# A decoder layer in fp32 on one core: the slices of the conditioning matrix get buffers and a queue of their own

## The chip, the cores and the metric

The kernel runs on one NeuronCore of a Trainium2 chip. The metric is the device time of one execution in microseconds (us); lower is better. The engines are TensorE (PE, with its weight loads PEld), VectorE (DVE), ScalarE (ACT), GpSimd (POOL) and SyncE (SP). Each runs its own list of instructions strictly in order, and they wait for one another through semaphores. Transfers between HBM and SBUF run on 16 DMA engines; they are put on a queue by the engine that issues them, here nearly always SP.

## The reference

One decoder layer on 256 tokens of width 2048, all in float32, with a conditioning vector c. What matters here:

```python
mod = silu(c) @ w_ada + b_ada              # 2048 x 12288: shift1, scale1, gate1, shift2, scale2, gate2
h   = RMSNorm(x) * (1 + scale1) + shift1
p   = h @ w_in                             # retention q,k,v,g | HGRN2 q,f,i,g | branch gates A, B
yA  = (LN_head(Retention(rope(q), rope(k), v)) * silu(g)) @ w_ret_o
yB  = (RMS_head(HGRN2(silu(q), f, i)) * silu(g)) @ w_hg_o
x   = x + gate1 * ((sigmoid(gA) * yA + sigmoid(gB) * yB) @ w_out)
h2  = RMSNorm(x) * (1 + scale2) + shift2
u   = causal_depthwise_conv3(h2 @ w_up);  a, b = split(u)
x   = x + gate2 * ((silu(a) * b) @ w_down)
out = RMSNorm_final(x)
```

## The kernel before

**Weights.** Every weight matrix is read once, in pieces of two k-tiles by 512 columns: 128 partitions by 1024 floats, 512 KB. A piece goes through one chain, which is called a weight step below. SP loads it into a buffer `raw` (`load`, L160). ACT rounds it to the format float32r, `wh` (L169). DVE subtracts, `wl = raw - wh` (L174), which ends the use of `raw`. TensorE multiplies with `wh` and `wl` (L191 to L193, L204 to L206, L848 and L849). `wh` and `wl` have four buffers each. The first eight steps, and a few more, have one k-tile (256 KB). There are 536 weight steps, and their order on DVE, ACT, SP and PE is fixed by the program.

**Conditioning.** `w_ada` stands transposed in memory with the bias appended, so that 128 outputs of `mod` are a 128 x 2049 slice, and TensorE has no part in it: DVE multiplies the slice with silu(c), which is kept on all partitions (`sc`), and sums along the row in the same instruction (L380). Each slice is loaded in two halves, of 1024 and of 1025 columns. One half, its load and its multiplication are called a dot here; there are 192 of them, with 100 MB in all: 64 for scale1 and shift1 (`ada1`), 32 for gate1, 64 for scale2 and shift2 (`ada2`), 32 for gate2. Small ACT instructions (L389 to L392, L400) put the two sums together. The halves of a dot use the same buffers `raw` as the weights, eight in all, and the same queue of SP:

```python
raw = self.wp.tile([P, m, w], F32, name=f"raw_{self.n}", tag="raw", bufs=8)   # load, L159
self.pin(self.nc.sync.dma_start(out=raw, in_=src))
```

**Order of the work.** The main program walks through the matrix products: twelve groups of columns of `w_in` for the attention branches (with the dots of `ada1` between them, since h needs them tile by tile), then `wb`, `wab`, `whg`, `wret`, `wout`, then 22 groups of `wup`, then `wdown`. Beside it run generators as background work: the recurrences (`hgrn`, `retention`), `gate_cols` and `ada2`. After each weight step `pump` lets them go on by a share of time that `pace` sets. So in program order gate1 and `ada2` are spread over the stages from `wb` to `wout`, and gate2 over `wup`.

The instructions are not issued in program order, though. While the program is built, a scheduler goes through it and writes the list of each engine: an instruction that has its inputs and a free buffer may be put ahead of others that are waiting, and earlier code has precedence. Only instructions that went through `pin` in the parts marked `ordered` (the start, and the passage from `wout` to the first group of `wup`) keep their program order. Loads on one queue stand in the order in which buffers come free for them.

**POOL** does next to nothing: it clears two tiles of each HGRN2 half, `at` (L486) and `kt` (L510), and issues two loads of `decay` (L593).

Of the kernel before, what the change touches and what calls it, by code (L numbers as in the profile page):

```python
# [12 lines left out]
F32 = mybir.dt.float32  # L13
# [3 lines left out]
ALU = mybir.AluOpType  # L17

P = 128
D = 2048  # L20
T = 256
NT = T // P
KT = D // P
# [9 lines left out]
RESIDENT = 2  # L33
ADA_EVERY = 11
LAG = 1
NOSYNC = mybir.DependencyInfo(mybir.DependencyClass.NoSync, mybir.DependencyReason.DATA)
SMALL = 70

# [4 lines left out]
GW = 2 * G  # L43
# [11 lines left out]
class Kernel:  # L55
    def __init__(self, ctx, tc, a):
        self.tc, self.nc, self.a = tc, tc.nc, a
        self.consts = ctx.enter_context(tc.tile_pool(name="consts", bufs=1))
        self.wp = ctx.enter_context(tc.tile_pool(name="wp", bufs=1))
        self.sb = ctx.enter_context(tc.tile_pool(name="sb", bufs=1))  # L60
        self.ps = ctx.enter_context(tc.tile_pool(name="ps", bufs=1, space=bass.MemoryType.PSUM))

        self.back = [deque(), deque()]
        self.rate = [0.0, 0.0]
        self.credit = [0.0, 0.0]
        self.n = 0

        self.ordered = True
# [87 lines left out]

    def load(self, src, m, w):
        self.n += 1
        raw = self.wp.tile([P, m, w], F32, name=f"raw_{self.n}", tag="raw", bufs=8)  # L159
        self.pin(self.nc.sync.dma_start(out=raw, in_=src))  # L160
        return raw

    def upper(self, src, m, w):
# [207 lines left out]
        self.pin(ins)  # L371
        return ins

    def ada_dot(self, src):

        nc = self.nc
        part = self.small([P, 2], name="dot", bufs=6)
        for u, w in enumerate((GW, D + 1 - GW)):
            raw = self.load(src[:, u * GW : u * GW + w], 1, w)
            self.pin(nc.vector.scalar_tensor_tensor(raw[:, 0, :], raw[:, 0, :], 1.0, self.sc[:, u * GW : u * GW + w], ALU.mult, ALU.mult, accum_out=part[:, u : u + 1]))  # L380
            yield 1.15
        return part

    def scale_shift(self, name, k, sc, sh, gn):

        act = self.nc.scalar.activation
        kk = slice(k, k + 1)
        part = yield from self.ada_dot(self.a[name][k, 0])
        self.pin(act(sc[:, kk], part[:, 0:1], AF.Identity, bias=part[:, 1:2]))  # L389
        self.pin(act(sc[:, kk], gn[:, kk], AF.Identity, bias=gn[:, kk], scale=sc[:, kk]))  # L390
        part = yield from self.ada_dot(self.a[name][k, 1])
        self.pin(act(sh[:, kk], part[:, 0:1], AF.Identity, bias=part[:, 1:2]))  # L392

    def gate_cols(self, name):
        gate = self.consts.tile([P, KT], F32, name=name)
        self.gate[name] = gate
        for k in range(KT):
            kk = slice(k, k + 1)
            part = yield from self.ada_dot(self.a[name][k])
            self.nc.scalar.activation(gate[:, kk], part[:, 0:1], AF.Identity, bias=part[:, 1:2])  # L400

    def ada2(self):
# [236 lines left out]
    def run(self):  # L639
# [12 lines left out]
        def act(k):  # L652
            return hT[k // 2][:, k % 2, :]

        def ada1(k):
            yield from self.scale_shift("ada1", k, s1, t1, self.gn1)
            if k % 2 == 0:
                hT[k // 2] = self.blk([P, 2, 2 * T], F32R, name="hT")
                if k:
                    ins = self.times(k, 2, rx_sb)  # L660
                    self.tc.add_manual_dep(ins.ins, start.ins.name, NOSYNC, reason="after the start")
            self.modulated(act(k), self.xT[k // 4][:, k % 4, :], k, s1, t1)
# [50 lines left out]
        while min(done) < KT:  # L713
            if work > SMALL and not small:
# [3 lines left out]
                self.start(self.lower_bound())  # L718
            have = min(KT, 2 + int((work - LAG) / ADA_EVERY))
            m = have - done[g]  # L720
# [267 lines left out]
```

## Time and profile before

| | before |
|---|---|
| median of 3 runs | 1580.73 us (1579.52 to 1589.53) |
| profiled execution, own time | 1580.22 us |
| its span, first to last instruction | 1578.4 us |
| PE busy | 1545.5 us (98%) |
| DVE busy | 1174.7 us (74%) |
| ACT busy | 839.8 us (53%) |
| POOL busy | 5.2 us |
| moved by DMA | 382.91 MB, 243 GB/s over the span |
| granted TensorE clock | 0.995 |

Busy time is the union of an engine's instructions. An engine that waits shows in the tables as idle time before an instruction, with the engine or transfer that ended the wait. L numbers are lines of the kernel before.

### The profile page before, as it was taken

What the parts mean: (1) busy time and instruction counts of PE and PEld (TensorE: products, weight loads), DVE (VectorE), ACT (ScalarE), POOL (GpSimd) and SP (SyncE); (2) the same over time, 40 slices, a digit from 0 to 9 for tenths busy, and PEclk for the clock granted to TensorE, in tenths of its full rate; (3) what the DMA queues carried; (4) which work ended last, traced back from release to release, by engine and by line L of the source; (5) the groups of instructions that cost most, each with busy time, mean ns of one, the idle gap of its engine ahead of it and who ended that gap; (6) DMA issues with size and microseconds to landing.
All of it is one profiled execution on the core that took longest, in us unless ns stands there. A gap on an engine that the chain in (4) does not pass through costs nothing.

```text
span 1578.4 us, 27236 instructions
## 1 busy us (share of the span) xinstructions
PE 1545.5 (98%) x10804; PEld 1439.9 (91%) x10804; DVE 1174.7 (74%) x1615; ACT 839.8 (53%) x1203; POOL 5.2 (0%) x10
## 2 busy tenths in 40 slices
PE   7999999999999999989999999999999999999997
PEld 6999999888999999989988888888888889999997
DVE  6899986997988866678758777777677768445444
ACT  5655455667755543344446555555555557434342
POOL 0000000000000000000000000000000000000000
PEclk9999999999999999999999999999999999999999
DMA  9999996887876778889847777777676666666661
GB/s 317 338 326 340 323 323 210 273 282 234 274 244 223 258 260 291 270 261 325 324 139 238 234 240 232 228 228 226 222 243 211 225 191 187 176 188 185 183 179 54
DMA packets 110019, 382.91 MB, mean 243 GB/s; under 512 B 12866, under 2 KB 13506, under 8 KB 109892
## 3 DMA queue, kind: packets, MB, share of 16 engines
q1 hardware_dynamic: 109440, 380.31, 74.1%
q8 instruction: 84, 1.38, 0.4%
q0 software_dynamic: 160, 0.79, 0.2%
q14 instruction: 43, 0.35, 0.1%
q10 hardware_dynamic: 292, 0.08, 0.0%
HBM read 379.04 MB, written 2.10 MB: 241 GB/s over the span
## 4 chain that ended last, share of the span: by engine, by line
PE 84%; DMA 7%; DVE 6%; issue 2%; ACT 1%; DVEq 0%; ACTq 0%; SPq 0%
PE pg L848 10%; PE po L848 10%; PE pg L206 9%; PE pg L204 9%; PE pg L205 9%; PE pg L849 5%; PE po L849 5%; DMA raw<-in_ada 5%; PE po L206 4%; PE po L204 4%; PE po L205 4%; PE pg L191 3%; PE pg L192 3%; PE pg L193 3%; DVE wl L174 3%
## 5 line engine op out<-in xcount | busy, mean ns | idle before, releaser
L174 DVE TENSOR_TENSOR wl<-raw,wh 128x1024 fp32r<-128x1024 f32 (+1 forms) x536 | 632.1, 1190 | 217.1 <-ACT wh L169 216.3
L169 ACT ACTIVATE wh<-raw 128x1024 fp32r<-128x1024 f32 (+1 forms) x536 | 544.9, 1029 | 416.6 <-PE pg L205 157.3
L380 DVE SCALAR_TENSOR_TENSOR raw<-raw,sc 128x1024 f32<-128x1024 f32 x192 | 234.2, 1224 | 131.5 <-DMA raw<-in_gate 66.9
L206 PE MATMUL pg<-hT,wl 128*128 128x256 f32 x896 | 254.1, 284 | 2.7 <-DVE wl L174 2.7
L204 PE MATMUL pg<-hT,wh 128*128 128x256 f32 x896 | 256.1, 286 | 0.1
L205 PE MATMUL pg<-hT,wh 128*128 128x256 f32 x896 | 253.5, 283 | 0.0
L848 PE MATMUL pg<-h2T,wh 128*128 128x512 f32 x704 | 247.1, 396 | 1.8 <-DVE h2T L365 1.8
L848 PE MATMUL po<-h2T,wh 128*128 128x512 f32 x704 | 244.6, 394 | 0.0
L849 PE MATMUL pg<-h2T,wl 128*128 128x256 f32 x704 | 196.2, 279 | 0.0
L849 PE MATMUL po<-h2T,wl 128*128 128x256 f32 x704 | 195.0, 277 | 0.0
L206 PEld LDWEIGHTS pg<-hT,wl 128*128 128x128 f32 x896 | 171.7, 192 | 3.7 <-DVE wl L174 3.7
L204 PEld LDWEIGHTS pg<-hT,wh 128*128 128x128 f32 x896 | 172.0, 192 | 1.2 <-ACT wh L169 0.6
L205 PEld LDWEIGHTS pg<-hT,wh 128*128 128x128 f32 x896 | 171.9, 192 | 0.3
L848 PEld LDWEIGHTS pg<-h2T,wh 128*128 128x128 f32 x704 | 133.1, 189 | 33.0 <-DVE h2T L365 2.0
L848 PEld LDWEIGHTS po<-h2T,wh 128*128 128x128 f32 x704 | 132.0, 188 | 30.6
L849 PEld LDWEIGHTS pg<-h2T,wl 128*128 128x128 f32 x704 | 133.3, 189 | 0.1
L849 PEld LDWEIGHTS po<-h2T,wl 128*128 128x128 f32 x704 | 132.2, 188 | 0.0
L191 PE MATMUL pg<-wh,hT 128*128 128x512 f32 x256 | 100.7, 393 | 0.0
L192 PE MATMUL pg<-wl,hT 128*128 128x512 f32 x256 | 100.0, 390 | 0.7 <-DVE wl L174 0.7
L193 PE MATMUL pg<-wh,hT 128*128 128x512 f32 x256 | 99.7, 390 | 0.0
L204 PE MATMUL po<-gs,wh 128*128 128x256 f32 x352 | 99.6, 283 | 0.0
L205 PE MATMUL po<-gs,wh 128*128 128x256 f32 x352 | 99.6, 283 | 0.0
(207 smaller groups left out, 2739.4 us busy)
## 6 DMA issues: line engine op xcount, KB each, us to landing
raw<-in_wup SPq DMA_DIRECT2D x176, 512.0 KB, 4.5
raw<-in_wdown SPq DMA_DIRECT2D x88, 512.0 KB, 3.9
raw<-in_wa SPq DMA_DIRECT2D x80, 512.0 KB, 5.6
raw<-in_ada SPq DMA_DIRECT2D x64, 512.5 KB, 5.4
raw<-in_ada SPq DMA_DIRECT2D x64, 512.0 KB, 5.3
raw<-in_wab SPq DMA_DIRECT2D x64, 512.0 KB, 4.8
raw<-in_gate SPq DMA_DIRECT2D x32, 512.5 KB, 4.3
raw<-in_wb SPq DMA_DIRECT2D x32, 512.0 KB, 5.4
```

Of the source, the lines that this page charges most:

```text
L169: self.pin(self.nc.scalar.activation(wh, raw, AF.Copy))
L174: self.last = self.nc.vector.tensor_tensor(wl, raw, wh.bitcast(F32), ALU.subtract)
L191: nc.tensor.matmul(ps[t], lhsT=hi, rhs=wh, start=first, stop=False)
L192: nc.tensor.matmul(ps[t], lhsT=hi, rhs=wl, start=False, stop=False)
L193: nc.tensor.matmul(ps[t], lhsT=lo, rhs=wh, start=False, stop=last)
L204: nc.tensor.matmul(out, lhsT=wh[:, cs], rhs=hi, start=opens, stop=False, skip_group_check=True)
L205: nc.tensor.matmul(out, lhsT=wh[:, cs], rhs=lo, start=False, stop=False, skip_group_check=True)
L206: nc.tensor.matmul(out, lhsT=wl[:, cs], rhs=hi, start=False, stop=last, skip_group_check=True)
L380: self.pin(nc.vector.scalar_tensor_tensor(raw[:, 0, :], raw[:, 0, :], 1.0, self.sc[:, u * GW : u * GW + w], ALU.mult, ALU.mult, accum_out= ...
L848: nc.tensor.matmul(ps[j], lhsT=wh[:, cs], rhs=act, start=kt == 0, stop=False)
L849: nc.tensor.matmul(ps[j][:, :T], lhsT=wl[:, cs], rhs=act[:, :T], start=False, stop=kt == KT - 1)
```

## The change

The halves of the dots get a pool of their own, `ada`, with three buffers. The pool `raw` has five buffers left, for the weights. The halves are listed ahead by `dot_plan`; when a dot is about to be multiplied, `dot_rows` first issues the loads of the next two, on the queue of GpSimd. In the part marked `ordered` at the start the first eight dots are still loaded by SP, the first half of each slice into a buffer of `raw`, the second into one of `ada`. The multiplication is the same; the lines of the changed kernel are 34 higher in this part (L414 for L380, L208 for L174, L163 and L169 for the loads).

```diff
--- before.py
+++ after.py
@@ -33,6 +33,7 @@
 RESIDENT = 2
 ADA_EVERY = 11
 LAG = 1
+AHEAD = 2
 NOSYNC = mybir.DependencyInfo(mybir.DependencyClass.NoSync, mybir.DependencyReason.DATA)
 SMALL = 70
 
@@ -59,6 +60,8 @@
         self.wp = ctx.enter_context(tc.tile_pool(name="wp", bufs=1))
         self.sb = ctx.enter_context(tc.tile_pool(name="sb", bufs=1))
         self.ps = ctx.enter_context(tc.tile_pool(name="ps", bufs=1, space=bass.MemoryType.PSUM))
+        self.plan = self.dot_plan()
+        self.fetched = deque()
 
         self.back = [deque(), deque()]
         self.rate = [0.0, 0.0]
@@ -156,8 +159,39 @@
 
     def load(self, src, m, w):
         self.n += 1
-        raw = self.wp.tile([P, m, w], F32, name=f"raw_{self.n}", tag="raw", bufs=8)
+        raw = self.wp.tile([P, m, w], F32, name=f"raw_{self.n}", tag="raw", bufs=5)
         self.pin(self.nc.sync.dma_start(out=raw, in_=src))
+        return raw
+
+    def load_dot(self, src, w, engine):
+        self.n += 1
+        raw = self.wp.tile([P, D + 1 - GW], F32, name=f"ada_{self.n}", tag="ada", bufs=AHEAD + 1)[:, :w]
+        self.pin(engine.dma_start(out=raw, in_=src))
+        return raw
+
+    def dot_plan(self):
+
+        for name, n in (("ada1", 2), ("gate1", 0), ("ada2", 2), ("gate2", 0)):
+            for k in range(KT):
+                for i in range(max(n, 1)):
+                    src = self.a[name][k, i] if n else self.a[name][k]
+                    for u, w in enumerate((GW, D + 1 - GW)):
+                        yield (name, k, i, u), src[:, u * GW : u * GW + w], w
+
+    def dot_rows(self, key):
+
+        if self.ordered and not self.fetched:
+            got, src, w = next(self.plan)
+
+            raw = self.load_dot(src, w, self.nc.sync) if got[3] else self.load(src, 1, w)[:, 0, :]
+        else:
+            while len(self.fetched) <= AHEAD:
+                got = next(self.plan, None)
+                if got is None:
+                    break
+                self.fetched.append((got[0], self.load_dot(got[1], got[2], self.nc.gpsimd)))
+            got, raw = self.fetched.popleft()
+        assert got == key, (got, key)
         return raw
 
     def upper(self, src, m, w):
@@ -371,13 +405,13 @@
         self.pin(ins)
         return ins
 
-    def ada_dot(self, src):
+    def ada_dot(self, name, k, i=0):
 
         nc = self.nc
         part = self.small([P, 2], name="dot", bufs=6)
         for u, w in enumerate((GW, D + 1 - GW)):
-            raw = self.load(src[:, u * GW : u * GW + w], 1, w)
-            self.pin(nc.vector.scalar_tensor_tensor(raw[:, 0, :], raw[:, 0, :], 1.0, self.sc[:, u * GW : u * GW + w], ALU.mult, ALU.mult, accum_out=part[:, u : u + 1]))
+            raw = self.dot_rows((name, k, i, u))
+            self.pin(nc.vector.scalar_tensor_tensor(raw, raw, 1.0, self.sc[:, u * GW : u * GW + w], ALU.mult, ALU.mult, accum_out=part[:, u : u + 1]))
             yield 1.15
         return part
 
@@ -385,10 +419,10 @@
 
         act = self.nc.scalar.activation
         kk = slice(k, k + 1)
-        part = yield from self.ada_dot(self.a[name][k, 0])
+        part = yield from self.ada_dot(name, k)
         self.pin(act(sc[:, kk], part[:, 0:1], AF.Identity, bias=part[:, 1:2]))
         self.pin(act(sc[:, kk], gn[:, kk], AF.Identity, bias=gn[:, kk], scale=sc[:, kk]))
-        part = yield from self.ada_dot(self.a[name][k, 1])
+        part = yield from self.ada_dot(name, k, 1)
         self.pin(act(sh[:, kk], part[:, 0:1], AF.Identity, bias=part[:, 1:2]))
 
     def gate_cols(self, name):
@@ -396,7 +430,7 @@
         self.gate[name] = gate
         for k in range(KT):
             kk = slice(k, k + 1)
-            part = yield from self.ada_dot(self.a[name][k])
+            part = yield from self.ada_dot(name, k)
             self.nc.scalar.activation(gate[:, kk], part[:, 0:1], AF.Identity, bias=part[:, 1:2])
 
     def ada2(self):
```

The scheduler makes a new list from this for each engine. The list of PE is the same but for 14 matmuls that stand a few places off. DVE, ACT and POOL have other lists.

On DVE, at the start of the program, the multiplications of the second k-tile of h stood like this before (`wl_291` is the first weight step of that tile, `hT_198` the tile, `raw_285` the last half of a slice that it needs):

```order
L380 SCALAR_TENSOR_TENSOR raw_285,dot_281<-raw_285,sc 128x1025
L370 TENSOR_TENSOR xT_94<-xT_94,rx_sb 128x512 x2
L370 TENSOR_TENSOR xT_95<-xT_95,rx_sb 128x512
L353 TENSOR_TENSOR hT_198<-h_294,hT_198 128x256
L174 TENSOR_TENSOR wl_291<-raw_288,wh_290 128x512
```

In the changed kernel the same place of DVE's list reads:

```order
L414 SCALAR_TENSOR_TENSOR ada_285,dot_281<-ada_285,sc 128x1025
L414 SCALAR_TENSOR_TENSOR ada_387,dot_386<-ada_387,sc 128x1024
L414 SCALAR_TENSOR_TENSOR ada_389,dot_386<-ada_389,sc 128x1025
L387 TENSOR_TENSOR hT_198<-h_294,hT_198 128x256
L208 TENSOR_TENSOR wl_291<-raw_288,wh_290 128x512
```

Two dots of the third k-tile, `ada_387` and `ada_389`, the first that POOL loads, now stand ahead of the weight step `wl_291`.

Further on, on DVE, ahead of the last weight steps of the branch gates (`wl_6533` before is the same step as `wl_6537` in the change, the 205th), the list had dots of `ada2` between the weight steps:

```order
L174 TENSOR_TENSOR wl_6468<-raw_6465,wh_6467 128x1024
L380 SCALAR_TENSOR_TENSOR raw_6659,dot_6625<-raw_6659,sc 128x1025
L174 TENSOR_TENSOR wl_6503<-raw_6500,wh_6502 128x1024
L380 SCALAR_TENSOR_TENSOR raw_6696,dot_6695<-raw_6696,sc 128x1024
L174 TENSOR_TENSOR wl_6533<-raw_6530,wh_6532 128x1024
L380 SCALAR_TENSOR_TENSOR raw_6729,dot_6695<-raw_6729,sc 128x1025
```

In the change the dots at this place are the last of gate2 (`ada_12409` to `ada_12799`), and weight steps alone follow:

```order
L414 SCALAR_TENSOR_TENSOR ada_12409,dot_12685<-ada_12409,sc 128x1024
L208 TENSOR_TENSOR wl_6472<-raw_6469,wh_6471 128x1024
L414 SCALAR_TENSOR_TENSOR ada_12557,dot_12685<-ada_12557,sc 128x1025
L208 TENSOR_TENSOR wl_6507<-raw_6504,wh_6506 128x1024
L414 SCALAR_TENSOR_TENSOR ada_12686,dot_12926<-ada_12686,sc 128x1024
L414 SCALAR_TENSOR_TENSOR ada_12799,dot_12926<-ada_12799,sc 128x1025
L208 TENSOR_TENSOR wl_6537<-raw_6534,wh_6536 128x1024
L208 TENSOR_TENSOR wl_6570<-raw_6567,wh_6569 128x1024
```

So all 192 dots stand ahead of the 205th weight step now; before, 125 of them did, and the last stood between two steps of `wup`. Counted in the two lists, the dots ahead of the 107th weight step are 64 before and 95 in the change; ahead of the 210th they are 128 and 192.

POOL's list, which had only the clearing of `at` and `kt` and the loads of `decay`, has 184 loads of dots now. Where the first HGRN2 half is cleared (`at_3393`, `kt_3480`; dots of `ada2` around them) it reads:

```order
L169 DMA ada_4971<-in_ada 128x1025
L169 DMA ada_5028<-in_ada 128x1024
L520 MEMSET at_3393 128x1024
L544 MEMSET kt_3480 128x1024
L169 DMA ada_5096<-in_ada 128x1025
L169 DMA ada_5165<-in_ada 128x1024
```

Before, these two clearings were the first work in POOL's list; 91 loads stand ahead of them now, and other loads behind them.

## The prediction

> **What bounds the kernel now.** I read the page's busy times and slices first, then the table by stages, then who waits for whom. On the page, TensorE is busy nearly all the time, DVE is fullest in the first third, and the DMA engines are fullest there too:
>
> ```profile
> span 1578.4 us, 27236 instructions
> PE 1545.5 (98%) x10804; PEld 1439.9 (91%) x10804; DVE 1174.7 (74%) x1615; ACT 839.8 (53%) x1203; POOL 5.2 (0%) x10
> ...
> DVE  6899986997988866678758777777677768445444
> ...
> DMA  9999996887876778889847777777676666666661
> GB/s 317 338 326 340 323 323 210 273 282 234 274 244 223 258 260 291 270 261 325 324 139 238 234 240 232 228 228 226 222 243 211 225 191 187 176 188 185 183 179 54
> ```
>
> The span leaves TensorE 1578.4 - 1545.5 = 32.9 us idle. The table by stages says where; its last two columns are the busy share of the DMA engines and what they moved:
>
> ```profile
> core 0: us, PE busy (x) PEld busy (x) DVE busy (x) ACT busy (x) POOL busy (x), PEclk, DMA share, GB/s
> 0.00:42.00 42.00, 33.02 (x148) 26.72 (x149) 30.04 (x56) 21.89 (x38) 0.20 (x4) 0.96 0.92 320
> 42.00:283.00 241.00, 240.24 (x1720) 227.34 (x1719) 205.86 (x265) 137.04 (x195) 1.91 (x2) 1.00 0.90 307
> 283.00:623.00 340.00, 337.30 (x2455) 315.87 (x2454) 284.07 (x389) 201.31 (x285) 3.12 (x4) 1.00 0.78 260
> 623.00:726.00 103.00, 94.91 (x771) 92.83 (x770) 76.01 (x89) 40.93 (x56) 0.00 (x0) 1.00 0.83 270
> 726.00:830.00 104.00, 101.27 (x808) 99.62 (x807) 75.16 (x106) 48.69 (x70) 0.00 (x0) 0.97 0.75 260
> 830.00:1250.00 420.00, 420.00 (x2423) 367.28 (x2422) 321.84 (x493) 237.66 (x362) 0.00 (x0) 1.00 0.72 231
> 1250.00:1578.00 328.00, 318.76 (x2490) 310.25 (x2489) 181.75 (x222) 152.25 (x202) 0.00 (x0) 0.99 0.58 169
> ```
>
> Start and end hold 9.0 + 9.2 us, which no dot's load can remove. Only 0.8 + 2.7 + 8.1 us are left between 42 and 726 us, and 2.7 us around the second norm. The waits show whose they are:
>
> ```profile
> DVE raw L380 <- DMA raw<-in_gate: 66.9, 33, 4.8
> DVE raw L380 <- DMA raw<-in_ada: 64.4, 44, 4.5
> ...
> PEld pg L206 <- DVE wl L174: 13.8, 15, 2.0
> PE pg L206 <- DVE wl L174: 10.7, 14, 1.8
> ```
>
> DVE waits 131 us for halves of dots, but only 10.7 us of it comes through to TensorE as a late `wl`. **This is a kernel bound by TensorE with little to win**: all of the time that late dots cost is about 11 us, 0.7%.
>
> **What the change moves.** The waits are small; the move in the order is large. Where the weight steps stand today is shown by the table of L174 alone (busy time of DVE, count):
>
> ```profile
> 0.00:42.00 42.00, 7.43 (x10) 0.96 0.92 320
> 42.00:283.00 241.00, 103.79 (x96) 1.00 0.90 307
> 283.00:623.00 340.00, 123.54 (x104) 1.00 0.78 260
> ```
>
> And the same for the dots, L380, which leave two records each:
>
> ```profile
> 0.00:42.00 42.00, 12.51 (x21) 0.96 0.92 320
> 42.00:283.00 241.00, 65.48 (x108) 1.00 0.90 307
> 283.00:623.00 340.00, 78.53 (x128) 1.00 0.78 260
> ```
>
> So 106 weight steps and 64 dots are done by 283 us, 210 steps and 128 dots by 623 us. In the changed list 95 dots stand ahead of the 107th step and all 192 ahead of the 210th. DVE runs its list in order, so TensorE can't get the 107th step before 31 more dots have been loaded and multiplied, nor the 210th before 64 more. The pace that `pump` sets holds in program order only; what held the dots back in the list was the common ring on SP.
>
> **Term A, bytes up to 283 us: +20 us.** 31 dots are 31 x 0.525 = 16.3 MB more. The engines moved 307 GB/s at a share of 0.90, so 341 GB/s at a full share. Their idle share is 0.08 x 42 + 0.10 x 241 = 27.5 us, room for 9.4 MB. The other 6.9 MB take 6.9 / 0.341 = 20 us in which weights come late. The best slice of the page (340 GB/s) says the same ceiling. Bounds: nothing, if two queues together draw 103.7 MB in 283 us, 366 GB/s, which no row shows; 16.3 / 0.341 = 48 us, if the idle share can't be used.
>
> The Trainium skill bears on this term: "DMA: Bandwidth & Descriptors", section "Issuing engines are not separate DMA queues", says that transfers issued from different engines run on the same 16 DMA engines and that a second issuing engine saves only issue time. By that rule term A stays at 20 us; without it, it could be nothing. No run here has two loaded queues.
>
> **Term B, the ring of three from 283 to 623 us: +32 us.** Here bytes fit: 33 more dots are 17.3 MB, 51 us, and 0.22 x 340 = 75 us are idle. DVE is the tight one. A dot costs it 1.225 + 0.085 = 1.31 us:
>
> ```profile
> L174 DVE TENSOR_TENSOR wl<-raw,wh 128x1024 fp32r<-128x1024 f32 (+1 forms) x104 | 124.6, 1211 | 7.3 <-ACT wh L169 7.0
> L380 DVE SCALAR_TENSOR_TENSOR raw<-raw,sc 128x1024 f32<-128x1024 f32 x64 | 78.1, 1225 | 45.5 <-DMA raw<-in_ada 33.6 <-DMA raw<-in_gate 11.8
> ...
> L380 DVE DVE_READ_ACCUMULATOR raw<-raw,sc 128x1 f32 x64 | 5.5, 85 | 0.0
> ...
> L471 DVE TENSOR_SCALAR f<-f 128x1024 f32<-128x1024 f32 x1 | 0.7, 689 | 0.0
> ```
>
> The change has 192 - 95 = 97 dots here against 64, so 33 x 1.31 = 43 us more on 284.1: 327 of 340 us, which leaves 13 us for every wait. Now the loads. With three buffers the load of dot n+2 can only be issued when dot n-1 is multiplied. What a load on POOL's queue takes from issue to landing is shown by two transfers alone; beside them SP's:
>
> ```profile
> raw<-in_wa SPq DMA_DIRECT2D x80, 512.0 KB, 5.6
> ...
> raw<-in_ada SPq DMA_DIRECT2D x64, 512.0 KB, 5.3
> ...
> raw<-in_wa SPq DMA_DIRECT2D x32, 256.0 KB, 5.0
> ...
> decay<-in_decay POOLq DMA_DIRECT2D x2, 384.0 KB, 7.0
> ```
>
> From 256 to 512 KB SP's loads grow by 0.6 us, so 7.0 us for 384 KB becomes 7.3 us for a dot. Ahead of it between dot n-1 and dot n+2 stands what DVE has to do meanwhile, taken from the changed list with each instruction's duration in the trace: of the 96 places of this stage 61 hold less than 7.3 us, and are short by 136 us together. A wait serves the three loads in flight at once, so a third of it, 45 us, is DVE waiting. 13 us are free, and 45 - 13 = 32 us come through to TensorE. Bounds: nothing with the 5.3 us of SP's queue (9 us of waiting, under the 13); with 7.0 x 512 / 384 = 9.3 us, 89 - 13 = 76 us. I take 7.3, as nearest to the only row of that queue.
>
> The same sum for 0 to 283 us gives 25 us of waiting. DVE has 283 - 236 = 47 us free there, less 31 x 1.31 = 41 us: 6 us. So 19 us come through, in the same stage and by the same late dots as the 20 us of term A; they are not added.
>
> **Term C, after 623 us: -8 us.** No dot is left, so the 8.1 us between 623 and 726 go. From 830 us TensorE is busy 420 of 420 us, and losing DVE's dots there gives nothing; the weights that would be late next come from SP with 0.28 of the DMA idle.
>
> **Edits at nothing.** Five buffers instead of eight: a weight holds its buffer for 5.6 us of loading, about 1 us of `wh` and 1.2 us of `wl`, some 8 to 10 us with waits, so five give a step every 2 us; TensorE takes 340 / 104 = 3.3 us a step. So 5 x 3.3 = 16 us may pass before a buffer is missed; a hold longer than that would cost TensorE a fifth of the excess at each step. POOL's 184 issues take 0.6 us each and lie beside everything. The clearing of `at` and `kt` (0.96 us each) stands among the loads: it waits for ACT, and the loads behind it wait too. The last load ahead of it is issued when 96 dots are done, and the first use of `at` on DVE has 104 dots ahead of it, so 8 dots or 8 x 340 / 97 = 28 us lie between, and I cost it at nothing; if ACT frees the buffer later than that, each microsecond over it is one of TensorE.
>
> At the start two dots from POOL now stand ahead of `wl_291`. The load of the second, `ada_389`, takes the buffer of `ada_276`, which is multiplied here at 25.20 us; the four weight steps from `wl_291` on start at 31.38:
>
> ```profile
> 25.20 1.22 DVE L380 SCALAR_TENSOR_TENSOR raw<-raw,sc 128x1025 f32<-128x1025 f32 x1
> ...
> 31.38 2.49 DVE L174 TENSOR_TENSOR wl<-raw,wh 128x512 fp32r<-128x512 f32 x4
> ```
>
> 25.2 + 1.3 + 7.3 + 1.3 and 0.4 for the tile of h make 35.5 us, so `wl_291` comes 4 us late. That is inside the 20 us of term A, whose weights are late anyway.
>
> **Sum.** 20 + 32 - 8 = +44 us on the profiled execution's own time of 1580.2 us, which is 0.5 us under the median of the runs shown: **1624 us**, 2.8% slower.
>
> **Rivals.**
> 1. *The loads fit, not slower.* If POOL's loads land in 5.3 us like SP's, term B is nothing; if moreover two queues draw 366 GB/s, term A is nothing too, and C and the 2.7 us of term B's stage are won: 1580.2 - 10.8 = 1569 us. It decides from 366 GB/s up to 283 us. For it: SP, which issues everything today, waits 197 us for multiplied dots, and weights stand behind those waits:
>
> ```profile
> SPq L160 <- DVE raw L380: 197.0, 174, 4.1
> ```
>
> Against it: the share is 0.90 to 0.92 already. Chance 0.07; with the wins at the start as well, over 1% faster, 0.02.
> 2. *Bytes alone.* Landing is quick, but the ceiling holds: 1580.2 + 20 - 8 = 1592 us. Against it: 7.0 us for less than a dot. Chance 0.08. The Trainium skill has a formula for it, in "DMA: Bandwidth & Descriptors", section "Anatomy of one DMA": about 2.0 us plus the bytes at 436 GB/s on GpSimd's path, for a dot an estimate of 3.2 us. By that rule term B would be nothing; the 7.0 us of `decay` speak against it.
> 3. *POOL's descriptors wait for DVE.* If an instruction of DVE in progress holds up the issue on POOL, each load lands up to 1.2 us later, at 8.5 us. Term B becomes 70 - 13 = 57 us, the first stage 48 - 6 = 42 us: 1580.2 + 42 + 57 - 8 = 1671 us. For it: DVE would be busy 96% of the time. Against it: in this trace only instructions like L471 run at double rate (689 ns for 1024 columns, against 1211 for `wl`), and there are seven. Chance 0.15. The Trainium skill tells of this in "SBUF — State Buffer", section "Who interferes with whom": a two-port mode of DVE shuts GpSimd out, while an instruction with two inputs in SBUF hinders only GpSimd's reads. By that rule the dots and `wl` would not do it.
>
> That the dots are not pulled ahead at all is excluded: the list is what the engine runs.
>
> **How the numbers follow.** The forecast (1600 to 1655) has 0.68, the rivals 0.09, 0.08 and 0.15. About 1% is what a measurement of this kernel tells from no change. Faster by over 1% (under 1565) needs nearly all of TensorE's idle time: 0.02. Within 1%: rival 1 and rival 2, with 1592 inside and its spread partly outside: 0.13. Slower: 0.85. The range reaches from rival 2 (1590) to rival 3 (1671, taken to 1672), which leaves out rival 1 below and larger landings above.
>
> **What would show it.** TensorE's idle time from 0 to 623 us grows from 12.5 to some 60 us, behind late `wl`, with DVE waiting for `ada` loads. The DMA share is 0.95 or more for the first 300 us. No dot is left after about 670 us, DVE has the weights alone there, and the stage of `wret` and `wout` runs without idle TensorE. Loads on POOL's queue land in about 7 us. Wrong it would be by landings under 6 us, by more than 345 GB/s in the first stage, or by an ACT that waits for dots and holds up `wh`, which I have not priced.

## The result and the profile after

| | median us | all executions | ratio to before (95% interval) |
|---|---|---|---|
| before | 1580.79 | 1579.52 to 1589.53 (4) | |
| changed | 1640.00 | 1633.19 to 1646.93 (4) | 1.0363 (1.0304 to 1.0421) |

The change makes the kernel 3.6% slower: 59 us by the medians, where 44 us were forecast. The profiled execution took 1633.2 us against 1580.2, so 53 us of it can be followed in the trace.

The page after: busy times, and the slices of DVE, of the DMA engines and of the bytes they moved.

```profile
span 1631.4 us, 27318 instructions
PE 1563.5 (96%) x10804; PEld 1452.5 (89%) x10804; DVE 1183.2 (73%) x1615; ACT 842.1 (52%) x1203; POOL 102.2 (6%) x194
...
DVE  6799989899898987656557776666766669445454
...
DMA  8999999888887789756764666666666666666662
GB/s 312 363 335 319 340 331 351 299 272 284 296 272 246 264 308 308 263 183 184 236 180 149 198 190 191 185 194 191 191 188 191 192 187 189 183 182 185 186 183 91
```

The DMA row stands at 8 or 9 through the twelfth slice, where the row before fell to 6 in the seventh, and from the 18th slice on hardly anything but weights is left (mostly 180 to 195 GB/s). POOL has 102 us of work, nearly all of it the issues of 184 loads. The table by the stages of the prediction:

```profile
core 0: us, PE busy (x) PEld busy (x) DVE busy (x) ACT busy (x) POOL busy (x), PEclk, DMA share, GB/s
0.00:42.00 42.00, 31.55 (x131) 25.47 (x132) 28.58 (x54) 20.05 (x38) 4.04 (x11) 0.92 0.89 315
42.00:283.00 241.00, 228.99 (x1597) 213.48 (x1596) 219.80 (x300) 123.93 (x185) 39.62 (x76) 0.99 0.96 339
283.00:623.00 340.00, 318.23 (x2197) 293.46 (x2196) 301.82 (x429) 204.41 (x305) 50.14 (x92) 0.97 0.84 281
623.00:726.00 103.00, 91.76 (x723) 90.30 (x722) 63.61 (x74) 37.90 (x45) 8.45 (x16) 0.96 0.77 253
726.00:830.00 104.00, 104.00 (x869) 104.00 (x868) 64.66 (x68) 46.26 (x54) 0.00 (x0) 1.00 0.64 201
```

TensorE is idle 10.5 + 12.0 + 21.8 = 44 us up to 623 us, where it was 12.5 before, and has done 3925 multiplications by then instead of 4323. Its clock fell too, which no idle time shows. The same program points, the 107th and the 210th weight step, now stand at about 310 and 687 us; here are the weight steps (L208) alone, DVE's busy time and count:

```profile
0.00:310.00 310.00, 111.71 (x107) 0.97 0.95 335
310.00:687.00 377.00, 124.96 (x104) 0.97 0.84 280
```

The chain of blame is read from the waits: who waited, for whom, us in total, times, longest.

```profile
POOL ada L169 <- DVE ada L414: 540.7, 174, 19.0
...
DVE ada L414 <- DMA ada<-in_ada: 34.0, 25, 3.4
DVE ada L414 <- DMA ada<-in_gate: 33.7, 26, 3.7
...
PEld pg L240 <- DVE wl L208: 21.1, 13, 3.5
PE pg L240 <- DVE wl L208: 18.3, 11, 3.2
```

POOL waits at nearly every load for a buffer of the ring (the three buffers of `ada`, used in turn); DVE waits for the load; TensorE waits for the `wl` that stands behind the dot on DVE. The loads themselves, beside SP's:

```profile
raw<-in_wa SPq DMA_DIRECT2D x80, 512.0 KB, 5.8
raw<-in_wab SPq DMA_DIRECT2D x64, 512.0 KB, 5.9
ada<-in_ada POOLq DMA_DIRECT2D x60, 512.5 KB, 6.3
ada<-in_ada POOLq DMA_DIRECT2D x60, 512.0 KB, 6.0
ada<-in_gate POOLq DMA_DIRECT2D x32, 512.5 KB, 6.1
```

POOL's loads land in 6.1 us, hardly later than SP's 5.8, and not in the 7.3 us of the forecast.

### The profile page after: what moved, and what is told of

It is laid out like the page before. It is cut to its first block, busy times and chain, and to the rows that moved or that the text cites. A ratio compares the mean times of both kernels' runs of the same rounds, so it can differ in the third digit from the quotient of the medians.

```text
span 1631.4 us, 27318 instructions
## 1 busy us (share of the span) xinstructions
PE 1563.5 (96%) x10804; PEld 1452.5 (89%) x10804; DVE 1183.2 (73%) x1615; ACT 842.1 (52%) x1203; POOL 102.2 (6%) x194
## 4 chain that ended last, share of the span: by engine, by line
PE 60%; issue 28%; POOL 5%; DVE 3%; DMA 2%; ACT 0%; POOLq 0%; DVEq 0%
PE pg L882 10%; PE po L882 10%; PE pg L240 6%; PE pg L239 6%; PE pg L238 6%; PE pg L883 5%; PE po L883 5%; POOL ada L169 5%; PE po L239 3%; PE po L240 3%; PE po L238 3%; DMA ada<-in_ada 1%; DVE wl L208 1%; DVE ada L414 1%; DMA ada<-in_gate 1%
## 5 line engine op out<-in xcount | busy, mean ns | idle before, releaser
L208 DVE TENSOR_TENSOR wl<-raw,wh 128x1024 fp32r<-128x1024 f32 (+1 forms) x536 | 634.5, 1191 | 322.2 <-ACT wh L203 321.5
L414 DVE SCALAR_TENSOR_TENSOR ada<-ada,sc 128x1025 f32<-128x1025 f32 (+1 forms) x188 | 228.6, 1222 | 68.6 <-DMA ada<-in_ada 34.0
L240 PE MATMUL pg<-hT,wl 128*128 128x256 f32 x896 | 259.7, 290 | 18.5 <-DVE wl L208 18.3
L238 PE MATMUL pg<-hT,wh 128*128 128x256 f32 x896 | 259.8, 290 | 1.0 <-DVE p L709 1.0
L239 PE MATMUL pg<-hT,wh 128*128 128x256 f32 x896 | 257.6, 287 | 0.0
L240 PEld LDWEIGHTS pg<-hT,wl 128*128 128x128 f32 x896 | 176.3, 197 | 21.2 <-DVE wl L208 21.1
L238 PEld LDWEIGHTS pg<-hT,wh 128*128 128x128 f32 x896 | 176.4, 197 | 2.2 <-issue 1.6
L239 PEld LDWEIGHTS pg<-hT,wh 128*128 128x128 f32 x896 | 176.3, 197 | 0.3
L225 PE MATMUL pg<-wh,hT 128*128 128x512 f32 x256 | 102.8, 401 | 7.2 <-DVE p L709 4.2
L227 PE MATMUL pg<-wh,hT 128*128 128x512 f32 x256 | 101.4, 396 | 0.0
```

Of the source, the lines that this page charges most:

```text
L208: self.last = self.nc.vector.tensor_tensor(wl, raw, wh.bitcast(F32), ALU.subtract)
L225: nc.tensor.matmul(ps[t], lhsT=hi, rhs=wh, start=first, stop=False)
L227: nc.tensor.matmul(ps[t], lhsT=lo, rhs=wh, start=False, stop=last)
L238: nc.tensor.matmul(out, lhsT=wh[:, cs], rhs=hi, start=opens, stop=False, skip_group_check=True)
L239: nc.tensor.matmul(out, lhsT=wh[:, cs], rhs=lo, start=False, stop=False, skip_group_check=True)
L240: nc.tensor.matmul(out, lhsT=wl[:, cs], rhs=hi, start=False, stop=last, skip_group_check=True)
```

## The experiments

All kernels below start from the changed one. To compare stages, I read from each profile when TensorE first multiplies with the `wl` of a given weight step, and subtract the time of that step before. The table gives this lateness in us; the 5th, 107th and 210th steps are the points at which the prediction's terms begin and end, and the 241st lies behind the stage of term C.

| kernel | median us | 5th | 107th | 210th | 241st |
|---|---|---|---|---|---|
| changed | 1640.0 | 3.2 | 27.4 | 64.2 | 53.6 |
| held | 1571.6 | 2.7 | 4.3 | 1.9 | -8.7 |
| lead48 | 1592.8 | 3.1 | 20.0 | 20.1 | 9.5 |
| place_half_bytes | 1584.8 | 1.6 | 7.9 | 16.0 | 5.4 |
| place_half_dve | 1639.9 | 2.2 | 26.9 | 63.3 | 52.7 |
| place_4_4 | 1604.8 | 3.5 | 21.6 | 35.8 | 25.2 |
| held_4_4 | 1574.7 | 2.9 | 6.8 | 4.4 | -6.2 |
| held_sp | 1585.8 | -0.8 | 15.2 | 12.4 | 1.7 |
| held_blk | 1570.0 | -0.7 | 1.0 | -1.4 | -12.1 |

The changed kernel's row already splits its 53 us: 27.4 up to the 107th step (term A), 36.8 from there to the 210th (term B), and 10.6 given back behind it (term C).

### held: the buffers and the queue, without the new order

An edge without a semaphore ties each dot on DVE behind the weight step emitted last, as a line for the scheduler only. The queue, the buffers and their numbers stay; 64 dots stand ahead of the 107th step and 125 ahead of the 210th, nearly as before (64 and 128).

```diff
-            self.pin(nc.vector.scalar_tensor_tensor(raw, raw, 1.0, ...))
+            ins = self.pin(nc.vector.scalar_tensor_tensor(raw, raw, 1.0, ...))
+            if not self.ordered and len(self.steps) > 0:
+                self.tc.add_manual_dep(ins.ins, self.steps[-1 - 0].ins.name, NOSYNC, ...)
```

> Only the order is undone: a dot may not stand on DVE ahead of the weight step that was written before it in the program (a dependency without a semaphore). The loads on GpSimd's queue, the three buffers and the five buffers of the weights stay as in the change. Ahead of the 107th weight step stand 64 dots and ahead of the 210th 125, as before the change (64 and 128). Theory of the order (the loss comes from 64 dots that are done ahead of the 210th step): about 1570 us, between 1565 and 1582, and less idle TensorE between 623 and 726 us than the 8 us of before. Rival, the queue and the buffers (loads of GpSimd land late and five buffers are too few, whatever the order): 1615 us or more.

1571.61 us; ratio to before 0.9939 (0.9919 to 0.9959). Its table by stages, from 42 us:

```profile
42.00:283.00 241.00, 238.95 (x1714) 226.40 (x1713) 204.91 (x266) 135.41 (x193) 30.88 (x57) 1.00 0.89 307
...
283.00:623.00 340.00, 339.11 (x2458) 317.35 (x2457) 285.79 (x390) 205.30 (x286) 35.48 (x66) 1.00 0.78 259
623.00:726.00 103.00, 103.00 (x860) 103.00 (x859) 86.38 (x101) 48.91 (x65) 11.81 (x23) 1.00 0.90 302
```

The multiplications of before are back (1714 and 2458, where before had 1720 and 2455), and TensorE has no idle time left between 623 and 726 us. **Undoing the order alone undoes the whole loss.** The buffers and the queue without the new order gain 0.6%.

### lead48: the order in part

The same edge, but to the weight step 48 back, so that dots may run up to 48 steps ahead: 88 stand ahead of the 107th step, 156 ahead of the 210th (the diff is against held).

```diff
-            if not self.ordered and len(self.steps) > 0:
-                self.tc.add_manual_dep(ins.ins, self.steps[-1 - 0].ins.name, NOSYNC, ...)
+            if not self.ordered and len(self.steps) > 48:
+                self.tc.add_manual_dep(ins.ins, self.steps[-1 - 48].ins.name, NOSYNC, ...)
```

> A dose between: a dot may stand at most 48 weight steps ahead of its place in the program; 88 dots stand ahead of the 107th step (64 before, 95 in the change) and 156 ahead of the 210th (128 and 192). Theory of the order: the lateness grows with the dots pulled ahead, so most of the loss at the 107th step (about 20 of 27 us) and under half of the part between the 107th and the 210th step, where 68 dots stand in place of 97 (64 before): 1595 to 1615 us. Rival, the queue and the buffers: like the change, 1630 us or more.

1592.78 us; ratio 1.0075 (1.0046 to 1.0105), a little under the expected range. The lateness follows the dots: 20.0 us at the 107th step with 24 dots more than before, and not a microsecond more up to the 210th, a stretch with 68 dots against 64 before and 97 in the changed kernel.

### place_half_bytes and place_half_dve: bytes or DVE's work

Both fix the changed kernel's order by a table that holds, for each dot, the weight step that it stands behind (95 and 192 dots ahead, as there). One loads half of each slice on POOL's queue and lets DVE multiply it twice, so DVE's work stays; the other loads all and lets DVE multiply half.

```diff
-        self.pin(engine.dma_start(out=raw, in_=src))
+        if engine is self.nc.gpsimd:
+            self.pin(engine.dma_start(out=raw[:, G:GW], in_=src[:, :G]))
...
+                once = raw[:, G:GW][:, None, :].to_broadcast([P, 2, G])
```

> The order of the change is kept by a table of places, and each load of GpSimd brings only the first 512 columns of its half; DVE multiplies them twice, with the same number of elements as in the change (so the conditioning values are not the reference's). Up to the 107th step 23 MB less are moved. Bytes (term A): the engines are no longer full in the first 300 us, and the lateness of TensorE at the 107th step falls from 27 us to under 10; total 1595 to 1612 us. Ring and landing (term B): landing gets shorter by a microsecond or two, and the part behind the 107th step falls from 37 us to about 20. If DVE's work alone is the limit: 1635 us, as in the change.

1584.83 us; ratio 1.0026 (0.9997 to 1.0055). That is below the expected 1595 to 1612 us: behind the 107th step only 8.1 us are added, not about 20.

```diff
+            n = w if self.ordered else G
+            ins = self.pin(nc.vector.scalar_tensor_tensor(raw[:, :n], raw[:, :n], 1.0, ...))
```

> The order of the change is kept by the same table, and the loads are whole, but DVE multiplies only the first 512 columns of each half that GpSimd loads (the conditioning values are not the reference's). That takes about 0.5 us off each of 184 dots, 45 us of DVE up to the 107th step and 50 us more up to the 210th. If bytes limit the first stage (term A): lateness at the 107th step stays at 20 to 27 us. If DVE limits: it falls under 8 us. Between the 107th and the 210th step DVE has some 50 us more for waits, so by term B at most a third of the 37 us is left. Total by bytes and ring: 1600 to 1620 us; by DVE alone: 1580 to 1590 us.

1639.9 us; ratio 1.037 (1.0336 to 1.0404), the changed kernel's time. The expectation for the stretch behind the 107th step fails: 36.4 of the 37 us are left there, not a third at most. The first stages of the two, place_half_bytes first:

```profile
42.00:283.00 241.00, 238.15 (x1706) 225.00 (x1704) 231.80 (x320) 135.27 (x200) 44.26 (x83) 1.00 0.85 271
```

```profile
42.00:283.00 241.00, 230.58 (x1592) 215.58 (x1593) 182.95 (x299) 123.40 (x184) 39.57 (x75) 0.98 0.95 338
```

With half the bytes DVE is fuller than in any kernel here (231.8 of 241 us), yet TensorE is nearly on time. With half of DVE's work and all the bytes it is as late as ever. So DVE's fullness is not the price. What became of DVE's time in term B's stretch is shown by the groups of dots, busy time, mean ns, then the idle time ahead of them and its cause; the changed kernel from 310 to 687 us first, place_half_dve from 310 to 690 behind it:

```profile
L414 DVE SCALAR_TENSOR_TENSOR ada<-ada,sc 128x1025 f32<-128x1025 f32 x49 | 59.9, 1222 | 25.4 <-DMA ada<-in_ada 13.1 <-DMA ada<-in_gate 12.0
L414 DVE SCALAR_TENSOR_TENSOR ada<-ada,sc 128x1024 f32<-128x1024 f32 x48 | 58.6, 1220 | 18.9 <-DMA ada<-in_gate 10.4 <-DMA ada<-in_ada 8.4
```

```profile
L428 DVE SCALAR_TENSOR_TENSOR ada<-ada,sc 128x512 f32<-128x512 f32 x97 | 66.3, 689 | 81.8 <-DMA ada<-in_ada 45.7 <-DMA ada<-in_gate 36.1
```

52 us less of multiplying became 38 us more of waiting for the same 97 loads, 82 us instead of 44. What paces this stretch is the load that can't start, not the engine that waits for it. But halving the bytes also makes each load land sooner:

```profile
ada<-in_ada POOLq DMA_DIRECT2D x120, 256.0 KB, 4.2
```

so place_half_bytes alone doesn't tell a full DMA from a ring that is too short.

### place_4_4: one buffer more for the dots

The changed kernel's order, with four buffers for dots, loaded three ahead, and four for weights. Bytes and DVE's work are whole.

```diff
-AHEAD = 2
+AHEAD = 3
-        raw = self.wp.tile([P, m, w], F32, name=f"raw_{self.n}", tag="raw", bufs=5)
+        raw = self.wp.tile([P, m, w], F32, name=f"raw_{self.n}", tag="raw", bufs=4)
```

> The order of the change is kept by the table; of the eight buffers four are for the weights and four for the dots, and the loads are issued three dots ahead. Theory of the ring (behind the 107th step the dots come as fast as three buffers can be filled again): the part of the lateness between the 107th and the 210th step falls from 37 us to 10 to 20 us, the part before it (27 us) hardly: 1610 to 1625 us. Theory of bytes (the DMA engines are the limit in both stages): about as in the change, 1632 to 1648 us. If four buffers are too few for the weights, it is over 1650 us; the next kernel tells that apart.

1604.81 us; ratio 1.0125 (1.0095 to 1.0156), a little under the range expected of the ring.

```profile
42.00:283.00 241.00, 231.70 (x1617) 216.88 (x1618) 223.84 (x304) 129.97 (x190) 40.65 (x77) 0.99 0.97 348
...
283.00:623.00 340.00, 329.17 (x2340) 306.26 (x2339) 314.44 (x447) 211.40 (x314) 53.90 (x99) 0.99 0.86 298
```

The two terms answer differently. Up to the 107th step the lateness falls only from 27.4 to 21.6 us, with the DMA engines nearly full at a share of 0.97. Two opposite effects are mixed in that. At the 47th step this kernel is later than the changed one, 16.2 us against 12.1; up to 142 us ACT waits 31.3 us for weights to land, against 7.0, so four buffers are short for the weights there. From the 47th step to the 107th it adds only some 5 us where the changed kernel adds 15, and the rate of the DMA engines from 142 to 304 us is 351 GB/s against 334. So the short ring has a part in the first stage too, and how much of term A is bytes alone isn't separated. From the 107th step to the 210th the added lateness falls from 36.8 to 14.2 us, although the loads land later, if anything:

```profile
ada<-in_ada POOLq DMA_DIRECT2D x60, 512.5 KB, 6.2
ada<-in_ada POOLq DMA_DIRECT2D x60, 512.0 KB, 6.6
```

So the fourth buffer takes 22.6 of term B's 36.8 us away: most of it was the ring. What the other 14.2 us are, no run here shows. DVE's waits for dots go the same way, to 24.3 us in all from 67.7:

```profile
DVE ada L427 <- DMA ada<-in_gate: 13.4, 18, 2.5
...
DVE ada L427 <- DMA ada<-in_ada: 10.9, 8, 4.5
```

### held_4_4: the price of four buffers for weights

held with the same two edits, so that what place_4_4 pays for its lost weight buffer is known.

> Four buffers for the weights and four for the dots, with the dots held at their place in the program. If four buffers are enough for the weights: as with five, 1568 to 1576 us. If not: over 1580 us, and the kernel with the order of the change and four buffers has to be read with that difference.

1574.67 us; ratio 0.9958 (0.9933 to 0.9983). It is 6.8 us late at the 107th step where held is 4.3, and stays 2.5 us behind held from there on: with this order the fifth buffer for weights is worth 2.5 us more than the fourth for dots, all of it in the first 60 steps or so. ACT's waits for weights to land show it: 28.2 us up to 142 us, against 4.8 in held.

### held_sp: own buffers, but SP's queue

held with the dots issued by SP, between the weights.

```diff
-                self.fetched.append((got[0], self.load_dot(got[1], got[2], self.nc.gpsimd)))
+                self.fetched.append((got[0], self.load_dot(got[1], got[2], self.nc.sync)))
```

> As the kernel with the held order, but the loads of the dots are issued by SP in place of GpSimd; buffers and order on DVE are the same. If the 11 us that the held order won between 623 and 726 us come from the buffers of their own (a dot's load no longer waits for a buffer in the ring of the weights): 1568 to 1575 us. If they come from the queue of its own (loads of dots pass the waiting loads of weights): the 8 us of idle TensorE in that stage come back, 1578 to 1586 us.

1585.82 us; ratio 1.0023 (0.9998 to 1.0048). The time is the one expected of the queue, but the idle TensorE that should explain it is not there. The stages say that two things are mixed:

```profile
42.00:283.00 241.00, 231.49 (x1615) 216.28 (x1614) 197.52 (x257) 124.09 (x176) 1.91 (x2) 0.99 0.90 303
...
623.00:726.00 103.00, 103.00 (x861) 103.00 (x860) 84.47 (x101) 47.05 (x61) 0.00 (x0) 1.00 0.91 301
```

From 623 to 726 us TensorE has no idle time here either, so that gain belongs to the buffers of their own and not to the queue. Up to the 107th step this kernel is 15.2 us late, though. SP's waits show with whom:

```profile
SPq L164 <- DVE wl L209: 865.4, 404, 12.6
SPq L170 <- DVE ada L416: 278.8, 161, 5.4
```

SP stands 278.8 us at loads of dots (L170) whose buffer is not free, and the weights are behind them in its list. With a queue of their own that wait stands on POOL, where only dots are behind it. So the time came out near before, but not because the queue does nothing: up to the 107th step it loses 11 us against held, and later it gains what held gains.

### held_blk: the start

held, with the first halves of the slices that are loaded at the start in buffers outside the ring of weights.

```diff
-            raw = self.load_dot(src, w, self.nc.sync) if got[3] else self.load(src, 1, w)[:, 0, :]
+            if got[3]:
+                raw = self.load_dot(src, w, self.nc.sync)
+            else:
+                raw = self.blk([P, w], name="first")
+                self.pin(self.nc.sync.dma_start(out=raw, in_=src))
```

> As the kernel with the held order, but the first halves of the slices that SP loads at the start get buffers of another pool, so that the first weights have the ring of five to themselves. If the 3 to 4 us that TensorE is late from the fifth step on come from that ring (a weight waits for the buffer of a dot): they go, 1566 to 1570 us. If they come from the later loads of the second k-tile's other halves: no change, 1570 to 1574 us.

1570.01 us; ratio 0.9920 (0.9893 to 0.9948), below both kernels. Its first 42 us, and held's behind it:

```profile
0.00:42.00 42.00, 32.79 (x149) 26.21 (x150) 30.83 (x57) 23.73 (x42) 3.50 (x10) 1.00 0.90 327
```

```profile
0.00:42.00 42.00, 30.60 (x135) 24.62 (x136) 27.85 (x52) 21.09 (x37) 2.44 (x8) 0.96 0.88 302
```

14 multiplications more are done by 42 us, and the lateness of 2.7 us at the 5th step is gone: SP issues the second slices' loads from 11.2 us on, and no longer from 17.7 us. But held_sp, with held's ring, is not late at the 5th step either (-0.8). What it lacks is the load that POOL issues at 19.7 us in held, among SP's loads. So either is enough to remove the 2.7 us, and the ring is not their only cause. By the medians held_blk and held are 1.6 us apart, within their spread; at the 241st step they are 3.4 us apart (-12.1 and -8.7).

## Why the prediction was right, and where it was not

The direction, the cause and the time within its range came out; 1640 lies 16 us above the 1624 forecast. By its steps:

**The move in the order.** Right, and shown: held, whose one edit undoes it, is 0.6% faster than before, where the changed kernel is 3.6% slower.

**Term A, bytes: forecast 20 us, measured 27.4.** The working asked for 87.4 + 16.3 = 103.7 MB by the 107th step. The changed kernel moved 310 x 0.335 = 103.9 MB by then, so the bytes are right; 341 GB/s was too much for the rate, since a share of 0.95 and 335 GB/s were held over the stage. The ring has a part in that: with one buffer more for dots the rate from 42 to 283 us is 348 GB/s instead of 339, and 5.8 us go although the weights then have a buffer less. That bytes alone would hold the stage is therefore not shown. The 366 GB/s of the first rival were not held over it, though single slices of 40 us came to 363 GB/s here and 379 in place_4_4. That is in agreement with the rule of the Trainium skill that was weighed there ("DMA: Bandwidth & Descriptors", section "Issuing engines are not separate DMA queues"): two loaded queues drew 339 GB/s from 42 to 283 us at a share of 0.96, one drew 307 at 0.90, which is nearly the same rate for a full share (353 and 341).

**Term B, the ring: forecast 32 us, measured 36.8.** The mechanism is shown by place_4_4 for 22.6 us of it. The sum behind the size was not right step by step. The landing was 6.1 us and not 7.3; the same count of places that hold less gives about 22 us of waiting with 6.1, and 44 were measured, so a third of the shortfall, or one landing time for every load, was too little. And the step "13 us are free" on DVE falls: place_half_dve freed 52 us of DVE there and TensorE stayed as late (36.4 us against 36.8), so free time of DVE is not to be taken off the waits. That the result was near is the luck of errors of opposite sign.

**What the sum lacked: the clock.** It held waits alone. Behind short waits TensorE also lost its clock, as the mean granted clock of the span shows, the changed kernel first, before behind it:

```profile
core 0: 1631.4 us, clock 0.985
```

```profile
core 0: 1578.4 us, clock 0.995
```

0.015 x 1631 = 24 us are lost to it, against 0.005 x 1578 = 8 us before; the clock record of the trace has ten pieces at half speed, most of them 3.4 or 6.8 us long, against three before, and by it 15.6 us more are lost. Seven of the ten begin in or just behind a wait of TensorE of 2.3 to 5.9 us; one wait of 2.7 us had none behind it. A stretch with one of them, which begins in a wait of 3.2 us for a late `wl`:

```profile
283.00:314.00 31.00, 26.26 (x167) 24.06 (x166) 26.39 (x35) 20.75 (x29) 6.58 (x11) 0.89 0.96 318
```

0.11 x 31 = 3.4 us, one piece of 6.8 us at half speed. It counts as busy, so TensorE's busy time rose by 18 us. Its idle time up to 623 us came to 44 us, not to the 60 that were forecast; another 11 us follow up to 726 us, because the late stage itself ends later. The Trainium skill describes this gate in "TensorE: Matmul & The Clock Gate", section "Part 1: The HAM clock gate": after an idle window of about 3.4 us the array runs at half rate. The trace agrees in the length of the pieces, but waits of 2.3 to 3.0 us, shorter than such a window, had pieces behind them too. Of the lateness, 6.8 us up to the 107th step and 10.2 us from there to the 210th are such lost time. How much of it would have been waited for anyway, since the weights were late, no run here separates.

**Term C: forecast -8 us, measured -10.6.** No dot is left after 675 us, and TensorE is busy 104.00 of 104.00 us from 726 us. held and held_sp give the same (-10.6 and -10.7) with dots in this stage, so buffers of their own are enough for the gain; an absence of dots is not needed for it.

**Edits at nothing.** The 4 us at the start were 3.2, but not by way of `ada_389` alone: held keeps the dots behind the weight steps and is 2.7 us late there too. held_blk and held_sp lose that by different ways, so its cause stays open between the ring of five and POOL's early load. Behind it five buffers cost hardly anything: held loses 1.6 us more up to the 107th step. POOL's issues (102.2 us for 194 instructions) and the two clearings cost nothing that shows. ACT, which the prediction left open, does wait for dots more (170 us up to 687 us, against 102 up to 623 before), but DVE waits for `wh` only 7.3 us there, against 30.3: no weight came late by it.

**The rivals.** The first, 1569 us, is what the change is worth without the move in the order: held gives 1571.6, held_blk 1570.0, though not by the 366 GB/s that the rival asked for. The second (1592, bytes alone) falls by place_4_4: the ring is a cost of its own. The Trainium skill's formula beside it ("DMA: Bandwidth & Descriptors", section "Anatomy of one DMA") gave an estimate of 3.2 us for a dot; 6.1 us were measured beside a loaded SP queue. The third, which asked for 8.5 us, falls by the same 6.1 us, with DVE busy 91% of the first stage.

**Left open.** The median lies 7 us above the profiled execution of the changed kernel. Executions of most kernels here, before included, lie in two groups some 8 us apart (held_blk: 1567.8 to 1578.0). In the traces of lead48, place_half_dve and held_blk such 8 us build up gradually behind the 300th weight step. TensorE is busy without a gap there, but held_blk does 568 multiplications in 100 us (from 900 us on) where held does 579. The cause is open.

## What to carry to other kernels

A buffer pool or a queue of its own takes away the wait that held work at its place, and a scheduler may then pull that work far ahead; read the new order on each engine, and count bytes and work up to the points where the critical stream must arrive, before looking at the stall that the edit removes. If the order must stay, an edge for the scheduler without a semaphore keeps it at no cost that shows here (held: -0.6% instead of +3.6%). DVE, waiting for loads from a short ring, was not relieved by less work of its own (place_half_dve); another buffer (place_4_4) helped, and so did half the bytes, which also land sooner (place_half_bytes).

## What the runs showed of the hardware

Loads on GpSimd's queue landed nearly as fast as SP's under the same load (6.1 against 5.8 us for 512 KB), with the DMA engines at a share of 0.84 to 0.96; the two loads of 384 KB from which the forecast took its 7.3 us said too much. Waits of TensorE of 2.3 to 5.9 us had pieces of 3.4 or 6.8 us at half clock behind them, a loss of 1.7 or 3.4 us more each. Two queues together drew up to 348 GB/s over 241 us, and 379 in one slice of 40 us (place_4_4).
